# RMSNorm and QKV projection on one core: another load order, another opening schedule, and the last two tiles stored by column chunk

## The chip, the cores and the metric

The kernel runs on one core of a Trainium2 chip. The core has a matrix engine (TensorE, in the profile PE for matmuls and PEld for weight loads), a vector engine (VectorE, DVE), a scalar engine (ScalarE, ACT), GpSimd (POOL) and a queue engine (SyncE, SP) that issues nearly all of this kernel's transfers. Every engine works through its own list of instructions in order; semaphores make one wait for another. Transfers from SP's queue are carried out by 16 DMA engines.

The metric is the device time of one execution in microseconds (us). A number of executions give a median.

## The reference, cut to what matters

```python
batch, n_heads, seq, head_dim = 8, 12, 1024, 64
dim = n_heads * head_dim                     # 768
x      (8, 1024, 768) f32;  gamma (768,);  w_qkv (768, 2304);  eps 1e-5

rms = np.sqrt(np.mean(x ** 2, axis=-1, keepdims=True) + eps)
x_norm = x / rms * gamma
return np.matmul(x_norm, w_qkv).astype(np.float32)
```

Each of the 8192 rows of x is divided by its root mean square, multiplied by gamma by column, and multiplied by a 768 by 2304 matrix.

## The kernel before, in words

**Tiling.** The 8192 rows are 64 x tiles of 128 rows. The inner dimension of 768 is six K blocks of 128. The 2304 output columns are four chunks of 512 and one of 256, at columns 0, 512, 1024, 1536 and 2048. One output chunk of one x tile is six matmuls that add up in one PSUM buffer; one x tile is 30 matmuls, the whole kernel 1920. Matmuls take bf16; x and the weights come as f32.

**Where the norm is done.** gamma is multiplied into the weights while they are converted to bf16 (`conv`, lines 160 to 168, on VectorE, ScalarE or GpSimd). The division by the root mean square is done when a chunk leaves PSUM (`evac`, lines 235 to 245, on VectorE or ScalarE): each row is multiplied by its reciprocal. `stat` (lines 180 to 186, ScalarE) sums the squares and takes the root, and `recip` (line 190, VectorE) inverts it.

**Transposing x.** A matmul needs x with its columns on the partitions. There are three ways in the kernel:

- `tr_half` and `cp_half` (lines 206 to 215), as `trA`, `trB`, `cpA`, `cpB` in the plan: TensorE transposes the f32 tile in two parts (K blocks 0 to 3, and 4 and 5), and VectorE or ScalarE copies them to bf16.
- `cast`, `tr` and `cp` (lines 176 to 200): VectorE casts the tile to bf16, TensorE transposes all six blocks, VectorE or ScalarE copies them out of PSUM.
- `cast` and `xbar` (line 219): VectorE casts, and SP issues a transfer that transposes.

Before, tiles 0 to 2 go the first way, tile 3 the second, and all others the third.

**Pieces of the weights.** The weights are loaded in 12 pieces. `PIECES` (line 12) gives each piece's first and last K block, first column and width. For columns 0 to 511 there is a piece of two K blocks and four of one; for 512 to 2047 pieces of three K blocks (768 KB); the last 256 columns are one piece. A piece lies in a staging buffer until all its K blocks are converted; pieces of one shape share up to four buffers (lines 115 and 157).

**The head.** The first six x tiles (`HEAD = 6`) are worked on together while the weights arrive. Their order is written out by hand: `HEAD_PLAN` (line 28) holds lines of a planned time, an operation, its arguments and an engine. `("mm", 0, 512, "345")` is: x tile 0, the chunk at column 512, K blocks 3, 4, 5. `LOADS` (line 17) holds the loads: `"w"` with a piece's number, `"x"` with a tile's, and `"t"`, the transposing transfer of a tile. All operations are sorted by planned time and then emitted (lines 316 and 317); the times set nothing but this order in each engine's list. `idle(n)` emits n matmuls on zeros (lines 275 to 278).

**After the head.** The other 58 tiles follow in a loop (lines 301 to 314): load, cast, transposing transfer, statistics, then 30 matmuls and five evictions, on VectorE and ScalarE in turn.

**Queues and buffers.** SP's queue holds every load of x and of weights, every transposing transfer and every store, in the order of the plan. Eight semaphores serve them in turn, so a transfer is issued only when the one eight places ahead of it has landed. All PSUM tiles, those of the transposes and the idle matmuls too, come from one pool of eight buffers in turn (line 128).

**Stores.** `evac_at` (lines 265 to 273) plans an eviction and its store. A tile's output is stored in three parts, `PARTS` (line 118): columns 0 to 1023, 1024 to 2047, and 2048 to 2303, each when all of its chunks are evicted. The last tile is stored chunk by chunk. In the head a store is planned at least 1.0 after its eviction and not before 21.85, just after the last entry of `LOADS`.

Of the kernel before, what the change touches and what calls it, by code (L numbers as in the profile page):

```python
# [8 lines left out]


HEAD = 6
PIECES = [(0, 2, 0, 512), (2, 3, 0, 512), (3, 4, 0, 512), (4, 5, 0, 512), (5, 6, 0, 512), (0, 3,
          512, 512), (3, 6, 512, 512), (0, 3, 1024, 512), (3, 6, 1024, 512), (0, 3, 1536, 512),
          (3, 6, 1536, 512), (0, 6, 2048, 256)]


LOADS = [
    (-9.00, "w", 0), (-8.99, "x", 0), (-8.98, "x", 1), (-8.97, "x", 2), (-8.96, "w", 1),
    (-8.95, "w", 2), (-8.94, "x", 3), (-8.93, "w", 3), (-8.92, "w", 4), (-8.91, "w", 5),
    (-8.90, "w", 6), (-8.89, "x", 4), (-8.88, "w", 7), (-8.87, "w", 8), (-8.86, "x", 5),  # L20
    (16.69, "t", 4), (16.70, "w", 9), (21.71, "t", 5), (21.72, "w", 10), (21.73, "w", 11),
    (21.74, "x", 6), (21.75, "x", 7),
]

EARLY = 3


HEAD_PLAN = [
    (4.99, "conv", 0, 0, "ACT"), (4.99, "conv", 0, 1, "DVE"), (5.95, "trA", 0), (5.99, "stat", 0),
    (6.82, "trB", 0), (7.04, "trB", 1), (7.25, "trA", 1), (7.26, "idle", 3), (7.38, "recip", 0),  # L30
    (7.39, "cpB", 1, "ACT"), (7.54, "cpA", 0, "DVE"), (7.83, "cpA", 1, "ACT"), (7.94, "trB", 2),
    (8.16, "trA", 2), (8.30, "cpB", 2, "DVE"), (8.45, "cpB", 0, "ACT"), (8.59, "mm", 0, 0, "01"),
    (8.70, "conv", 1, 2, "DVE"), (8.81, "stat", 2), (9.02, "mm", 1, 0, "01"),
    (9.18, "cpA", 2, "DVE"), (9.32, "conv", 2, 3, "POOL"), (9.45, "mm", 0, 0, "2"),
    (9.67, "mm", 1, 0, "2"), (9.92, "mm", 2, 0, "012"), (10.31, "cast", 3, "DVE"),
    (10.31, "stat", 3), (10.56, "mm", 0, 0, "3"), (10.78, "mm", 1, 0, "3"), (10.86, "recip", 2),
    (10.99, "mm", 2, 0, "3"), (11.02, "conv", 3, 4, "DVE"), (11.21, "tr", 3),
    (11.56, "mm", 0, 0, "4"), (11.65, "conv", 4, 5, "DVE"), (11.69, "cp", 3, "ACT"),
    (11.78, "mm", 1, 0, "4"), (12.00, "mm", 2, 0, "4"), (12.13, "recip", 3),
    (12.21, "mm", 0, 0, "5"), (12.43, "mm", 1, 0, "5"), (12.54, "stat", 1),  # L40
    (12.59, "evac", 0, 0, "DVE"), (12.64, "mm", 3, 0, "01234"), (13.67, "conv", 5, 0, "DVE"),
    (13.67, "conv", 5, 1, "POOL"), (13.72, "mm", 2, 0, "5"), (13.94, "mm", 3, 0, "5"),
    (14.10, "evac", 2, 0, "ACT"), (14.15, "recip", 1), (14.21, "mm", 0, 512, "0"),
    (14.31, "evac", 3, 0, "DVE"), (14.42, "mm", 1, 512, "0"), (14.62, "conv", 5, 2, "POOL"),
    (14.64, "mm", 2, 512, "0"), (14.79, "evac", 1, 0, "ACT"), (14.85, "mm", 0, 512, "1"),
    (15.07, "mm", 1, 512, "1"), (15.28, "mm", 2, 512, "1"), (15.50, "mm", 3, 512, "0"),
    (15.68, "conv", 6, 3, "DVE"), (15.68, "conv", 6, 4, "POOL"), (15.68, "conv", 6, 5, "ACT"),
    (15.72, "mm", 0, 512, "2"), (15.93, "mm", 1, 512, "2"), (16.15, "mm", 2, 512, "2"),
    (16.36, "mm", 3, 512, "12"), (16.67, "cast", 4, "DVE"), (16.67, "stat", 4),
    (16.80, "mm", 0, 512, "345"), (17.44, "mm", 1, 512, "345"), (18.06, "recip", 4),  # L50
    (18.09, "mm", 2, 512, "345"), (18.25, "evac", 1, 512, "ACT"), (18.68, "conv", 7, 0, "DVE"),
    (18.74, "mm", 3, 512, "345"), (18.94, "conv", 7, 1, "ACT"), (19.16, "conv", 7, 2, "DVE"),
    (19.39, "mm", 0, 1024, "0"), (19.60, "mm", 1, 1024, "0"), (19.64, "evac", 2, 512, "DVE"),
    (19.65, "evac", 3, 512, "ACT"), (19.82, "mm", 0, 1024, "12"), (20.25, "mm", 1, 1024, "12"),
    (20.39, "evac", 0, 512, "DVE"), (20.68, "mm", 2, 1024, "012"), (20.70, "conv", 8, 3, "ACT"),
    (20.70, "conv", 8, 4, "POOL"), (21.33, "mm", 3, 1024, "012"), (21.69, "cast", 5, "DVE"),
    (21.69, "stat", 5), (21.97, "mm", 0, 1024, "34"), (22.41, "mm", 1, 1024, "34"),
    (22.84, "mm", 4, 0, "012345"), (23.02, "conv", 8, 5, "ACT"), (23.08, "recip", 5),
    (24.13, "mm", 4, 512, "012345"), (24.29, "evac", 4, 0, "DVE"), (24.65, "conv", 9, 0, "POOL"),
    (24.65, "conv", 9, 1, "ACT"), (25.36, "conv", 9, 2, "ACT"), (25.43, "mm", 4, 1024, "012"),  # L60
    (25.59, "evac", 4, 512, "DVE"), (26.07, "mm", 0, 1024, "5"), (26.29, "mm", 1, 1024, "5"),
    (26.45, "evac", 0, 1024, "DVE"), (26.51, "mm", 2, 1024, "345"),
    (26.67, "evac", 1, 1024, "ACT"), (27.15, "mm", 3, 1024, "345"),
    (27.31, "evac", 2, 1024, "DVE"), (27.80, "mm", 4, 1024, "345"),
    (27.96, "evac", 3, 1024, "ACT"), (28.45, "mm", 5, 0, "012345"),
    (28.65, "evac", 4, 1024, "ACT"), (29.25, "conv", 10, 3, "POOL"),
    (29.25, "conv", 10, 5, "DVE"), (29.74, "mm", 5, 512, "012345"), (29.90, "evac", 5, 0, "DVE"),
    (30.20, "conv", 10, 4, "POOL"), (31.04, "mm", 5, 1024, "012345"),
    (31.20, "evac", 5, 512, "DVE"), (31.64, "conv", 11, 0, "ACT"), (31.64, "conv", 11, 4, "POOL"),
    (31.95, "conv", 11, 2, "DVE"), (32.12, "conv", 11, 5, "ACT"), (32.25, "conv", 11, 3, "DVE"),  # L70
    (32.33, "mm", 0, 1536, "012"), (32.55, "evac", 5, 1024, "DVE"), (32.98, "mm", 1, 1536, "012"),
    (33.30, "conv", 11, 1, "DVE"), (33.63, "mm", 2, 1536, "012"), (34.28, "mm", 3, 1536, "012"),
    (34.92, "mm", 4, 1536, "012"), (35.57, "mm", 5, 1536, "012"), (36.22, "mm", 0, 1536, "345"),
    (36.86, "mm", 1, 1536, "345"), (37.02, "evac", 0, 1536, "DVE"), (37.51, "mm", 2, 1536, "345"),
    (37.67, "evac", 1, 1536, "ACT"), (38.16, "mm", 3, 1536, "345"),
    (38.32, "evac", 2, 1536, "DVE"), (38.81, "mm", 4, 1536, "345"),
    (38.97, "evac", 3, 1536, "ACT"), (39.45, "mm", 5, 1536, "345"),
    (39.61, "evac", 4, 1536, "DVE"), (40.10, "mm", 0, 2048, "012345"),
    (40.26, "evac", 5, 1536, "ACT"), (40.76, "mm", 1, 2048, "012345"),
    (40.92, "evac", 0, 2048, "DVE"), (41.41, "mm", 2, 2048, "012345"),  # L80
    (41.57, "evac", 1, 2048, "DVE"), (42.07, "mm", 3, 2048, "012345"),
    (42.23, "evac", 2, 2048, "DVE"), (42.72, "mm", 4, 2048, "012345"),
    (42.88, "evac", 3, 2048, "DVE"), (43.38, "mm", 5, 2048, "012345"),
    (43.54, "evac", 4, 2048, "DVE"), (44.19, "evac", 5, 2048, "DVE"),
]
HEAD_END = 44.03


@with_exitstack
def kernel(  # L90
# [21 lines left out]
    MT = M // P  # L112
    NT = 512
    inv_k = 1.0 / float(K)
    PIECE_BUFS = {(k1 - k0, n): min(4, sum((q[1] - q[0], q[3]) == (k1 - k0, n) for q in PIECES))
                  for k0, k1, _, n in PIECES}

# [37 lines left out]
    def load_w(c):  # L155
        k0, k1, n0, n = PIECES[c]
        WF[c] = wst.tile([P, k1 - k0, n], f32, name=f"w_f{k1 - k0}_{n}", bufs=PIECE_BUFS[k1 - k0, n])
        nc.sync.dma_start(out=WF[c], in_=wv[:, k0:k1, n0:n0 + n])  # L158

    def conv(c, ko, eng):  # L160
        k0, k1, n0, n = PIECES[c]
        o, i, g = w_b[:, ko, n0:n0 + n], WF[c][:, ko - k0, :], g_sb[:, ko:ko + 1]
        if eng == "DVE":
            nc.vector.tensor_scalar(out=o, in0=i, scalar1=g, scalar2=None, op0=mult)  # L164
        elif eng == "ACT":
            nc.scalar.activation(out=o, in_=i, func=AF.Copy, scale=g, bias=0.0)  # L166
        else:
            nc.gpsimd.tensor_scalar(out=o, in0=i, scalar1=g, scalar2=1.0, op0=mult, op1=mult)  # L168
# [86 lines left out]
    def at(time, fn, *args):  # L255
        plan.append((time, len(plan), fn, args))
# [8 lines left out]
    def evac_at(time, t, n0, eng, gap):  # L265
        at(time, evac, t, n0, eng)
        h = part(n0)
        nl = min(NT, N - n0)
        left[t, h] = left.get((t, h), PARTS[h][1]) - nl
        if t == MT - 1:  # L270
            at(time + gap - 0.5, store, t, h, n0, nl)
        elif left[t, h] == 0:
            at(time + gap, store, t, h, *PARTS[h])
# [8 lines left out]
        at(time, {"x": load_x, "w": load_w, "t": xbar}[kind], n)  # L282
    at(0.0, idle, 18)
    at(2.8, gamma_in)
    at(2.81, idle, 28)
    ops = {"conv": conv, "cast": cast, "stat": stat, "recip": recip, "tr": tr, "cp": cp, "mm": mm, "idle": idle}
    for time, op, *args in HEAD_PLAN:
        if op == "evac":
# [10 lines left out]
    US = 6 * 0.2158 / 512  # L299
    now, flip = HEAD_END, 0  # L300
    for t in range(HEAD, MT):
# [51 lines left out]
```

## Time and profile before

| what | value |
|---|---|
| median of 7 executions | 389.51 us (389.13 to 389.89) |
| the profiled execution's own time | 389.73 us |
| its span, first to last instruction | 387.9 us |
| TensorE busy with matmuls | 379.8 us (98%) |
| VectorE, ScalarE, GpSimd busy | 153.9, 181.1, 7.5 us |
| moved by DMA | 119.91 MB, mean 309 GB/s |
| granted TensorE clock over the span | 1.000 |

The profile is of one execution. In a timeline, a line gives the start and the time that a group took, the engine and line of the kernel, the operation, what it writes and reads, how many there are, and in brackets how long the engine was idle before it and what ended that. Matmuls are pipelined: the time of a group holds a tail after its last start. "SPq" and the like are an engine's sequencer, which issues transfers. The chain that ended last is followed back from the last instruction, at each step to what released it. Some matmul records are missing from a trace.

### The profile page before, as it was taken

What the parts mean: (1) busy time and instruction counts of PE and PEld (TensorE: products, weight loads), DVE (VectorE), ACT (ScalarE), POOL (GpSimd) and SP (SyncE); (2) the same over time, 40 slices, a digit from 0 to 9 for tenths busy, and PEclk for the clock granted to TensorE, in tenths of its full rate; (3) what the DMA queues carried; (4) which work ended last, traced back from release to release, by engine and by line L of the source; (5) the groups of instructions that cost most, each with busy time, mean ns of one, the idle gap of its engine ahead of it and who ended that gap; (6) DMA issues with size and microseconds to landing.
All of it is one profiled execution on the core that took longest, in us unless ns stands there. A gap on an engine that the chain in (4) does not pass through costs nothing.

```text
span 387.9 us, 5512 instructions
## 1 busy us (share of the span) xinstructions
PE 379.8 (98%) x1956; PEld 195.1 (50%) x1994; DVE 153.9 (40%) x309; ACT 181.1 (47%) x362; POOL 7.5 (2%) x15
## 2 busy tenths in 40 slices
PE   8999999999999999999999999999999999999995
PEld 7444654554554554554554554554554554554552
DVE  2655524444333344333343433343433343433331
ACT  4762444444544444444444444544444544444531
POOL 0312000000000000000000000000000000000000
PEclk9999999999999999999999999999999999999999
DMA  8999999999999999999999999999999999999964
GB/s 269 390 277 383 325 373 336 384 344 329 329 284 316 288 313 306 290 325 306 291 311 293 309 318 304 289 314 306 304 276 338 302 308 299 270 341 294 297 241 190
DMA packets 89223, 119.91 MB, mean 309 GB/s; under 512 B 52326, under 2 KB 61292, under 8 KB 89196
## 3 DMA queue, kind: packets, MB, share of 16 engines
q1 hardware_dynamic: 89184, 119.56, 100.8%
q8 instruction: 15, 0.25, 0.3%
q14 instruction: 12, 0.10, 0.1%
q10 hardware_dynamic: 12, 0.00, 0.0%
HBM read 32.25 MB, written 75.50 MB: 278 GB/s over the span
## 4 chain that ended last, share of the span: by engine, by line
PE 93%; DMA 4%; issue 1%; SPq 0%; DVE 0%; ACT 0%
PE pm L229 93%; DMA w_f<-in_w_qkv_dram 4%; SPq L153 0%; DVE w_b L164 0%; ACT ot L245 0%; SPq L158 0%
## 5 line engine op out<-in xcount | busy, mean ns | idle before, releaser
L229 PE MATMUL pm<-w_b,xT 128*128 128x512 bf16 (+1 forms) x1882 | 371.9, 357 | 2.2 <-DVE w_b L164 0.2
L229 PEld LDWEIGHTS <-xT 128*128 128x128 bf16 x1920 | 187.7, 98 | 185.8 <-issue 0.5
L243 DVE TENSOR_SCALAR ot<-pm,rstd 128x512 f32<-128x512 f32 (+1 forms) x165 | 113.6, 694 | 200.4 <-PE pm L229 200.0
L245 ACT ACTIVATE ot<-pm,rstd 128x512 f32<-128x512 f32 (+1 forms) x155 | 100.2, 647 | 190.8 <-PE pm L229 154.5
L183 ACT ACTIVATE sq<-x_t 128x768 bf16<-128x768 f32 x64 | 53.4, 835 | 1.6 <-DMA x_t<-in_x_dram 1.6
L172 DVE CAST xb<-x_t 128x768 bf16<-128x768 f32 x61 | 33.2, 545 | 18.9 <-DMA x_t<-in_x_dram 18.9
L185 ACT ACTIVATE rms<-ssq,eps_sb 128x1 f32<-128x1 f32 x64 | 18.8, 294 | 2.1
L183 ACT ACTIVATION_READ_ACCUMULATOR sq<-x_t 128x1 f32 x64 | 12.3, 192 | 0.0
L190 DVE RECIPROCAL rstd<-rms 128x1 f32<-128x1 f32 x64 | 9.8, 154 | 3.2 <-ACT rms L185 3.2
L166 ACT ACTIVATE w_b<-w_f,g_sb 128x512 bf16<-128x512 f32 (+1 forms) x9 | 5.8, 669 | 5.3 <-DMA w_f<-in_w_qkv_dram 5.3
L168 POOL TENSOR_SCALAR w_b<-w_f,g_sb 128x512 bf16<-128x512 f32 (+1 forms) x9 | 6.8, 765 | 24.8 <-DMA w_f<-in_w_qkv_dram 15.8
L278 PE MATMUL pm<-warm 128*128 128x128 bf16 x49 | 5.5, 305 | 1.0 <-DVE eps_sb L137 1.0
L164 DVE TENSOR_SCALAR w_b<-w_f,g_sb 128x512 bf16<-128x512 f32 (+1 forms) x12 | 5.2, 450 | 2.9 <-DMA w_f<-in_w_qkv_dram 2.8
L278 PEld LDWEIGHTS <-warm 128*128 128x128 bf16 x49 | 5.0, 144 | 1.0 <-DVE eps_sb L137 1.0
L210 PE MATMUL pm<-ident_f,x_t 128*128 128x128 f32 x18 | 2.5, 277 | 0.9 <-DMA x_t<-in_x_dram 0.9
L210 PEld LDWEIGHTS pm<-ident_f,x_t 128*128 128x128 f32 x18 | 1.9, 141 | 1.3 <-DMA x_t<-in_x_dram 1.2
L172 DVE CAST xT<-pm 128x512 bf16<-128x512 f32 (+1 forms) x3 | 1.8, 600 | 1.9 <-PE pm L210 1.9
L174 ACT CAST xT<-pm 128x256 bf16<-128x256 f32 (+1 forms) x3 | 1.2, 445 | 1.8 <-PE pm L210 1.7
L140 ACT ACT_TABLE_LOAD x1 | 1.3, 1283 | 1.4 <-PEq L334 1.4
L174 ACT COPY xT<-pm 128x768 bf16<-128x768 bf16 x1 | 0.8, 798 | 0.3 <-PE pm L196 0.3
L261 DVE COPY g_sb<-pm 128x6 f32<-128x6 f32 x1 | 0.2, 164 | 1.8 <-PE pm L260 1.8
L196 PEld LDWEIGHTS <-xb 128*128 128x128 bf16 x6 | 0.4, 98 | 0.2
(13 smaller groups left out, 2.4 us busy)
## 6 DMA issues: line engine op xcount, KB each, us to landing
out_dram<-ot SPq DMA_DIRECT2D x126, 512.0 KB, 3.8
x_t<-in_x_dram SPq DMA_DIRECT2D x64, 384.0 KB, 4.1
out_dram<-ot SPq DMA_DIRECT2D x64, 128.0 KB, 3.2
w_f<-in_w_qkv_dram SPq DMA_DIRECT2D x7, 768.0 KB, 8.7
w_f<-in_w_qkv_dram SPq DMA_DIRECT2D x4, 256.0 KB, 7.0
out_dram<-ot SPq DMA_DIRECT2D x4, 256.0 KB, 2.0
xT<-xb SPq DMA_TRANSPOSE x60, 4.3
w_f<-in_w_qkv_dram SPq DMA_DIRECT2D x1, 512.0 KB, 3.7
```

The lines of the kernel that those rows point to most:

```text
L164: nc.vector.tensor_scalar(out=o, in0=i, scalar1=g, scalar2=None, op0=mult)
L166: nc.scalar.activation(out=o, in_=i, func=AF.Copy, scale=g, bias=0.0)
L168: nc.gpsimd.tensor_scalar(out=o, in0=i, scalar1=g, scalar2=1.0, op0=mult, op1=mult)
L172: nc.vector.tensor_copy(out=out, in_=in_)
L183: nc.scalar.activation(out=sq, in_=X[t], func=AF.Square, accum_out=ssq)
L185: nc.scalar.activation(out=rms, in_=ssq, func=AF.Sqrt, scale=inv_k, bias=eps_sb)
L190: nc.vector.reciprocal(out=r, in_=RS[t])
L210: nc.tensor.transpose(out=PT[t, h][:, ko - k0, :], in_=X[t][:, ko * P:(ko + 1) * P], identity=ident_f)
L229: nc.tensor.matmul(out=PM[t, n0][:, :nl], lhsT=XT[t][:, ko, :], rhs=w_b[:, ko, n0:n0 + nl], start=(b == 1), stop=(b == KO))
L243: nc.vector.tensor_scalar(out=o, in0=pm[:, :nl], scalar1=RS[t], scalar2=None, op0=mult)
L245: nc.scalar.activation(out=o, in_=pm[:, :nl], func=AF.Copy, scale=RS[t], bias=0.0)
L278: nc.tensor.matmul(out=wps, lhsT=warm, rhs=warm, start=True, stop=True)
```

## The change

The change replaces the tables of the head, lets x tiles 4 and 5 be transposed by TensorE, and stores one more tile by chunk. No function of the arithmetic is changed.

- **Load order.** x tiles 0 and 1 are loaded before the first piece of weights; x tile 3 moves ahead of piece 2. All head loads, x 6 and 7 too, stand at the front of SP's list; the two `"t"` entries are gone.
- **Pieces.** Columns 512 to 1023 come as three pieces of two K blocks (512 KB) instead of two of three. There are 13 pieces; no shape has more pieces than staging buffers, except that three-block pieces now number four, for four buffers.
- **Head order.** A new `HEAD_PLAN`: statistics of tiles 0 and 1 at once, first conversions on ScalarE and GpSimd, x tile 2's transposes between the first matmuls, tile 3's copy on VectorE, and `tr` and `cp` for tiles 4 and 5 (on VectorE and ScalarE).
- **Idle matmuls.** 28 after gamma's become 9, and 3 before the first matmuls become 13.
- **Stores.** The last two tiles, not the last one alone, are stored chunk by chunk. With the last entry of `LOADS` at -8.80, head stores are planned 1.0 after their eviction.

```diff
-PIECES = [(0, 2, 0, 512), (2, 3, 0, 512), (3, 4, 0, 512), (4, 5, 0, 512), (5, 6, 0, 512), (0, 3,
-          512, 512), (3, 6, 512, 512), (0, 3, 1024, 512), (3, 6, 1024, 512), (0, 3, 1536, 512),
-          (3, 6, 1536, 512), (0, 6, 2048, 256)]
+PIECES = [(0, 2, 0, 512), (2, 3, 0, 512), (3, 4, 0, 512), (4, 5, 0, 512), (5, 6, 0, 512), (0, 2,
+          512, 512), (2, 4, 512, 512), (4, 6, 512, 512), (0, 3, 1024, 512), (3, 6, 1024, 512), (0,
+          3, 1536, 512), (3, 6, 1536, 512), (0, 6, 2048, 256)]

 LOADS = [
-    (-9.00, "w", 0), (-8.99, "x", 0), (-8.98, "x", 1), (-8.97, "x", 2), (-8.96, "w", 1),
-    (-8.95, "w", 2), (-8.94, "x", 3), (-8.93, "w", 3), (-8.92, "w", 4), (-8.91, "w", 5),
-    (-8.90, "w", 6), (-8.89, "x", 4), (-8.88, "w", 7), (-8.87, "w", 8), (-8.86, "x", 5),
-    (16.69, "t", 4), (16.70, "w", 9), (21.71, "t", 5), (21.72, "w", 10), (21.73, "w", 11),
-    (21.74, "x", 6), (21.75, "x", 7),
+    (-9.00, "x", 0), (-8.99, "x", 1), (-8.98, "w", 0), (-8.97, "x", 2), (-8.96, "w", 1),
+    (-8.95, "x", 3), (-8.94, "w", 2), (-8.93, "w", 3), (-8.92, "w", 4), (-8.91, "w", 5),
+    (-8.90, "w", 6), (-8.89, "x", 4), (-8.88, "w", 7), (-8.87, "w", 8), (-8.86, "w", 9),
+    (-8.85, "x", 5), (-8.84, "w", 10), (-8.83, "w", 11), (-8.82, "w", 12), (-8.81, "x", 6),
+    (-8.80, "x", 7),
 ]
 HEAD_PLAN = [
+    (4.00, "stat", 0), (4.00, "trA", 0), (4.87, "trB", 0), (5.01, "cpA", 0, "DVE"),
+    (5.31, "trB", 1), (5.33, "stat", 1), (5.69, "cpB", 0, "DVE"), (5.74, "trA", 1),
+    (5.75, "idle", 13), (6.09, "cpB", 1, "DVE"), (6.49, "recip", 0), (6.72, "recip", 1),
+    (6.83, "conv", 0, 0, "ACT"), (6.83, "conv", 0, 1, "POOL"), (6.88, "cpA", 1, "DVE"),
+    (7.60, "mm", 0, 0, "0"), (7.82, "trA", 2), (7.83, "stat", 2), (8.25, "mm", 0, 0, "1"),
+    (8.39, "cpA", 2, "DVE"), (8.47, "mm", 1, 0, "01"), (8.50, "conv", 1, 2, "POOL"),
+    (8.90, "trB", 2), (9.13, "mm", 2, 0, "01"), (9.22, "recip", 2), (9.26, "cpB", 2, "ACT"),
+    (9.49, "cast", 3, "DVE"), (9.57, "mm", 0, 0, "2"), (9.62, "stat", 3), (9.78, "mm", 1, 0, "2"),
+    (10.00, "mm", 2, 0, "2"), (10.16, "conv", 2, 3, "DVE"), (10.21, "tr", 3),
+    (10.70, "mm", 0, 0, "3"), (10.83, "conv", 3, 4, "DVE"), (10.92, "mm", 1, 0, "3"),
+    (11.14, "mm", 2, 0, "3"), (11.31, "cp", 3, "DVE"), (11.37, "mm", 0, 0, "4"),
+    (11.59, "mm", 1, 0, "4"), (11.81, "mm", 2, 0, "4"), (11.87, "recip", 3),
+    (12.02, "mm", 3, 0, "01234"), (12.03, "conv", 4, 5, "DVE"), (12.85, "conv", 5, 0, "DVE"),
+    (13.10, "mm", 0, 0, "5"), (13.32, "mm", 1, 0, "5"), (13.33, "conv", 5, 1, "DVE"),
...
+    (14.40, "mm", 1, 512, "01"), (14.56, "conv", 6, 2, "DVE"), (14.83, "mm", 2, 512, "01"),
+    (14.86, "evac", 3, 0, "ACT"), (15.04, "conv", 6, 3, "DVE"), (15.26, "mm", 3, 512, "01"),
+    (15.52, "cast", 4, "DVE"), (15.55, "stat", 4), (15.69, "mm", 0, 512, "23"),
+    (16.12, "mm", 1, 512, "2"), (16.34, "tr", 4), (16.67, "mm", 1, 512, "3"),
+    (16.81, "cp", 4, "DVE"), (16.89, "mm", 2, 512, "23"), (17.32, "mm", 3, 512, "23"),
+    (17.37, "recip", 4), (17.42, "conv", 7, 5, "ACT"), (17.53, "conv", 7, 4, "DVE"),
+    (17.75, "mm", 4, 0, "012345"), (19.05, "mm", 4, 512, "0123"), (19.21, "evac", 4, 0, "DVE"),
+    (19.91, "mm", 0, 512, "45"), (19.96, "conv", 8, 2, "DVE"), (20.34, "mm", 1, 512, "45"),
...
+    (22.40, "conv", 9, 3, "POOL"), (22.57, "stat", 5), (22.72, "mm", 1, 1024, "012"),
+    (22.98, "cast", 5, "DVE"), (23.36, "mm", 2, 1024, "01"), (23.79, "tr", 5),
+    (23.90, "conv", 9, 4, "ACT"), (23.96, "recip", 5), (24.13, "mm", 2, 1024, "2"),
+    (24.35, "mm", 3, 1024, "012"), (24.45, "conv", 10, 2, "DVE"), (24.61, "cp", 5, "ACT"),
...
-HEAD_END = 44.03
+HEAD_END = 44.46
...
-        if t == MT - 1:
+        if t >= MT - 2:
             at(time + gap - 0.5, store, t, h, n0, nl)
...
-    at(2.81, idle, 28)
+    at(2.81, idle, 9)
```

## The prediction

> **What bounds the kernel now.** I read the chain that ended last first, then the matmul engine's timeline, then the queue's and the other engines' timelines over the head.
>
> The page's chain, and pieces of the chain in order of time (start, us, what):
>
> ```profile
> PE 93%; DMA 4%; issue 1%; SPq 0%; DVE 0%; ACT 0%
> ...
> 9.49 10.63 DMA w_f<-in_w_qkv_dram
> 20.12 0.03 issue
> 20.15 0.50 DVE w_b L164
> 20.64 0.04 issue
> 20.69 10.30 PE pm L229 x47
> ...
> 55.92 9.46 PE pm L229 x49
> 65.38 0.05 issue
> 65.43 9.46 PE pm L229 x49
> 74.89 0.05 issue
> 74.94 10.10 PE pm L229 x49
> ...
> 383.96 0.47 ACT ot L245
> ```
>
> Until 20.15 us weight loads end the chain, from 20.69 on only matmuls do. The three blocks from 55.92 to 85.09 are 29.17 us; with one record lost per block (1,882 records against 1,920 weight loads) they are 150 matmuls, five x tiles of 30, so a tile is 5.834 us and 64 tiles are 373.4 us. The same blocks repeat to the end, so there is no steady stall to win. TensorE's timeline over the head:
>
> ```profile
> 3.22 3.08 PE L278 MATMUL pm<-warm 128*128 128x128 bf16 x28
> 6.14 0.82 PE L210 MATMUL pm<-ident_f,x_t 128*128 128x128 f32 x6
> 7.90 0.87 PE L210 MATMUL pm<-ident_f,x_t 128*128 128x128 f32 x6 [0.93 <-DMA x_t<-in_x_dram]
> 8.61 0.33 PE L278 MATMUL pm<-warm 128*128 128x128 bf16 x3
> 8.93 0.85 PE L210 MATMUL pm<-ident_f,x_t 128*128 128x128 f32 x6
> 9.62 2.75 PE L229 MATMUL pm<-w_b,xT 128*128 128x512 bf16 x11
> 12.21 0.50 PE L196 MATMUL pm<-ident,xb 128*128 128x128 bf16 x6
> 12.54 7.93 PE L229 MATMUL pm<-w_b,xT 128*128 128x512 bf16 x35
> 20.69 29.56 PE L229 MATMUL pm<-w_b,xT 128*128 128x512 bf16 x152 [0.21 <-DVE w_b L164]
> ```
>
> Real matmuls begin at 9.62. After that only two things stand between them: tile 3's six transposes (12.21 to 12.54, 0.335) and one wait for piece 7. The last matmul before it starts near 20.10 and needs 0.216 (29.17/5, less six 256-wide ones at half the time, over 24: 5.834/27), so 20.31 to 20.69 is 0.38 lost. The account closes: 9.62 + 373.4 + 0.34 + 0.38 = 383.7, and the last eviction starts at 383.96. The span is 387.9 and its run 389.73, 0.22 above the median of 389.51; I count differences on the profiled execution and add them to the median.
>
> **When loads land.** With eight loads out, a load issues when the one eight places ahead has landed, so issue starts and waits give landings: w0 4.48 (ACT's first conversion), x0 5.37, x1 7.87, x2 8.81, w1 9.49, w2 10.17, x3 11.14, w3 at most 11.83, w4 12.52, w5 14.55, w6 16.55, x4 18.11, w7 20.14, w8 22.15, x5 23.11. I lay these against KB asked for so far (x 384, pieces 512, 256 or 768). The new order has the same totals at many places: x1 768 KB, by interpolation 5.1; w0 1280, 7.87; x2 1664, 8.81; w1 1920, 9.49; x3 2304, 10.5; w2 2560, 11.14; w3 2816, 11.8; w4 12.5; w5 3584, 13.9; w6 4096, 15.2; x4 16.2; w7 4992, 18.1; w8 20.1; w9 22.15; x5 23.1.
>
> **The change part by part.**
>
> *Order of loads and the first matmuls.* x0 and x1 are squared and transposed before w0 lands. Then ACT's conversion (0.72) gives block 0 at 8.59, and with 0.05 to TensorE (20.64 to 20.69 in the chain) the first matmul is at 8.65, not 9.62. GpSimd converts block 1 (0.69, longest row 0.99: at worst 8.9) and block 2 (9.55 to 10.24, at worst 10.54). TensorE does one matmul, 0.44 of x2's transposes, three matmuls, 0.22 of transposes to 10.24; VectorE's copy of x2's first half ends at 10.23, so the next five matmuls run 10.28 to 11.36, tile 3's transposes to 11.69 and, after w2's conversion (11.2 to 11.68), three more to 12.38. The conversion of w3 (11.87 to 12.35) opens block 4 at 12.40. At that point both kernels have done the same: x0 to x2 on blocks 0 to 3, and tile 3 transposed. Before reaches it at 12.54. So most of the 0.97 us at the first matmul is lost again to x2's transposes in the stream (0.66) and to the wait for w3: gain 0.14.
>
> *Tile 3's copy moves from ACT (0.80) to VectorE,* behind w3's conversion. No row has this copy on VectorE. Bounds: 0.56, the cast of as many elements from SBUF; and 0.955, from 0.69 for 512 and 0.425 for 256 f32 elements out of PSUM. I take 0.80, the same tile's row, between them: 12.35 to 13.15, when TensorE is free at 13.05, so 0.15 lost (0.56 loses nothing, 0.955 loses 0.30). VectorE's conversions of blocks 4 and 5 queue behind it, to 13.79: TensorE wants them at 14.28.
>
> [...]
>
> *Tiles 4 and 5 by TensorE.* Two more sets of six transposes in the stream: 2 x 0.335 = 0.67 lost. Their casts are ready: x4 lands at 16.2, cast by 17.3, transposes wanted at 17.5; x5 at 23.1, cast after two evictions by 24.8, wanted near 25.0. This is the thinnest cover; if VectorE is one 0.75 eviction later, up to 0.6 is added.
>
> *Two queue transposes removed.* In before, SP waits from 12.24 to 18.70 for tile 4's cast, and piece 9 stands behind it. This view by stage (PE, PEld, DVE, ACT, POOL, then clock, DMA share, GB/s) shows the price:
>
> ```profile
> 5.00:10.00 5.00, 4.06 (x36) 3.48 (x35) 1.43 (x4) 3.00 (x8) 0.00 (x0) 1.00 0.99 345
> 10.00:15.00 5.00, 4.95 (x28) 2.37 (x28) 3.68 (x10) 3.95 (x10) 1.08 (x2) 1.00 1.05 394
> 20.00:25.00 5.00, 4.79 (x22) 2.03 (x21) 2.92 (x6) 3.86 (x7) 0.69 (x1) 1.00 1.17 269
> 25.00:30.00 5.00, 5.00 (x25) 2.28 (x24) 3.22 (x5) 2.72 (x5) 0.85 (x2) 1.00 0.95 287
> ```
>
> From 20 to 30 the rate falls from 394 to 269 and 287. Yet TensorE is full there, so faster loads win nothing; worth 0. All 21 new loads issue with no buffer wait, and head stores, no longer held to 21.85, queue behind them.
>
> *Pieces of two blocks.* w7 lands at 18.1 and is wanted near 21, since tile 4's matmuls come first: the 0.38 stall goes. Next in line are w6's conversions, ready at 16.6 against 16.9; covered by 0.3.
>
> *Stores by chunk for the last two tiles.* Two more issues of 0.33 in SP's queue while it idles (next store at 380.14); the last tile's stores were in chunks already. From 370 to 380 the DMA share is 0.66, so nothing queues: 0, with ends of -0.2 (a larger store out of the way) and +0.2.
>
> Sum: -0.14 + 0.15 + 0.67 - 0.38 = **+0.30 us**: profiled 390.03, on the median 389.8, or +0.08%. A measurement here tells about 0.2% (0.78 us) from no change, so I forecast no change.
>
> **The rivals.**
>
> *Cold clock (slower).* Warm-up matmuls go from 28 + 3 to 9 + 13, with transposes between. In before the 28 take 3.08 us (0.11 each) and the later 3 only 0.33 with a pipeline tail of 0.22, so full speed came near 6.1, 5.1 us after TensorE's start. If full speed is not reached by 8.65 and needs about that long from there, 4 to 5 us run at half speed: 2.0 to 2.5 lost, less 0.17 of waiting; with +0.30, 391.6 to 392.1. It decides once the cold stretch after 8.65 passes 1.3 us. Against it: from 6.14 to 9.62 before ran almost only transposes and stayed at speed.
>
> [...]
>
> *Loads without the early lag (faster).* x1 took from 5.37 to 7.87 where x0 took 0.89. At the later 394 GB/s the stage from 5 to 10 would need 4.38 us: 0.62 earlier, hence +0.30 - 0.62, 389.2. With no lag at all x1's total lands at 6.26, 1.6 earlier; TensorE's own work then limits, block 4 opens near 11.0, and it is 388.4. For it: the rows show the lag only before 9 us, so it belongs to the start, which is what is reordered. Against: the same bytes are asked for at the same times.
>
> *VectorE late (slightly slower).* It now takes copies 3 and 4 and more conversions. Copy at 0.955 adds 0.15, tile 5's cast 0.6, and one eviction in front of w6's conversion 0.4: 390.0 to 390.9.
>
> **How the numbers follow.** Forecast 0.52, cold clock 0.13, loads earlier 0.2, VectorE late 0.15. Beyond 0.2% lie most of the earlier loads' far half (faster 0.15), the cold clock, half of VectorE late and 0.07 of unplanned waits in the forecast's tail (slower 0.28); 0.57 is left within. The range 388.8 to 391.0 leaves out the far ends of the first two rivals. The forecast's own range is 389.4 to 390.3.
>
> **What would show it.** First real matmul near 8.65, block 4 of x0 near 12.4, three groups of L196 transposes, no wait for weights after 13, tile 6 starting about 0.3 later, L174 or L172 rows for the copies. Wrong if warm-up spacing (0.11) goes on past 8.65, if weights land a microsecond off, or if TensorE has gaps between 13 and 45.

## The result and the profile after

| | before | after |
|---|---|---|
| median time, us | 389.3 (389.02 to 389.89, 38 executions) | 390.22 (389.57 to 392.37, 16 executions) |
| ratio | | 1.0025 (1.0018 to 1.0032) |
| the profiled execution: time / span | 389.73 / 387.94 | 390.0 / 387.85 |
| median span | 387.7 (102 executions of the later series) | 388.05 (28 executions of both) |
| time outside the span, mean | 1.79 | 2.11 |

The changed kernel is slower by 0.25%, about 0.9 us. A second series of the same two kernels gave 1.0016 (1.0007 to 1.0024). Both medians lie in the range, 0.2 to 0.4 above the forecast of 389.8; a loss beyond the 0.2% that the forecast kept to was measured in the first series, and one within it in the second. The two profiled spans differ by 0.1 only, the other way, and that is the puzzle that the runs below had to solve. The median spans differ by 0.35. By series it is less even: in the second the median spans differ by 0.1 (387.7 and 387.8); in the first, whose spans of before were not kept, times less the 1.79 and 2.11 outside the span differ by some 0.6.

The page's chain of the changed kernel, as shares of the span:

```profile
PE 96%; DMA 2%; issue 1%; ACT 0%; SPq 0%; ACTq 0%
```

The weight loads' share fell from 4 to 2: after 13 us no load ends the chain any more. TensorE's timeline over the head of the changed kernel (start, us, what, and in brackets the idle time ahead):

```profile
4.21 2.77 PE L210 MATMUL pm<-ident_f,x_t 128*128 128x128 f32 x12
6.78 1.15 PE L278 MATMUL pm<-warm 128*128 128x128 bf16 x13
8.41 0.38 PE L229 MATMUL pm<-w_b,xT 128*128 128x512 bf16 x1 [0.48 <-ACT w_b L166]
...
11.11 0.50 PE L196 MATMUL pm<-ident,xb 128*128 128x128 bf16 x6
11.55 5.77 PE L229 MATMUL pm<-w_b,xT 128*128 128x512 bf16 x26
17.16 0.50 PE L196 MATMUL pm<-ident,xb 128*128 128x128 bf16 x6
17.49 7.29 PE L229 MATMUL pm<-w_b,xT 128*128 128x512 bf16 x32
24.61 0.50 PE L196 MATMUL pm<-ident,xb 128*128 128x128 bf16 x6
24.95 25.25 PE L229 MATMUL pm<-w_b,xT 128*128 128x512 bf16 x131
```

The first real matmul is at 8.41, tiles 0 and 1 are transposed before it, there are three groups of six bf16 transposes, and the wait for piece 7 at 20.5 is gone. By stage (PE, PEld, DVE, ACT, POOL, then clock, DMA share, GB/s) the changed kernel shows

```profile
5.00:10.00 5.00, 4.47 (x32) 3.71 (x31) 2.91 (x8) 3.30 (x8) 1.34 (x2) 1.00 0.98 326
10.00:15.00 5.00, 5.00 (x28) 2.44 (x28) 3.81 (x10) 2.16 (x6) 0.04 (x1) 1.00 1.05 396
20.00:25.00 5.00, 5.00 (x30) 2.40 (x28) 4.12 (x8) 3.24 (x7) 1.36 (x2) 1.00 1.04 389
```

From 20 to 25 the loads run at 389 GB/s where before had 269. TensorE is full in both (5.00 against 4.79, and the 0.21 is the wait for piece 7), so the 120 GB/s buy nothing else.

**Where the time went.** From the first real matmul to the last one's start there are 373.33 us of matmuls, plus the transposes that stand between them, plus waits, which are what is left over; where a gap shows in TensorE's records, it agrees with them. Then come the tail (last matmul's start to the end of the span) and the time outside the span. In us:

| trace | first matmul | transposes in the stream | waits | sum of the three | tail | outside, mean of its executions |
|---|---|---|---|---|---|---|
| before | 9.62 | 0.34 | 0.38 | 10.3 | 4.29 | 1.79 |
| before, again | 9.45 | 0.34 | 0.65 | 10.4 | 4.28 | 1.80 |
| before, two tiles by chunk (part 3) | 8.97 | 0.34 | 1.32 | 10.6 | 3.91 | 1.80 |
| before, two by chunk and softer lead (part 6) | 8.69 | 0.34 | 0.97 | 10.0 | 3.94 | 1.78 |
| after | 8.41 | 1.66 | 0.20 | 10.3 | 4.25 | 2.11 |
| after, again | 7.85 | 1.66 | 0.72 | 10.2 | 4.26 | 2.13 |
| after, gamma later (part 2) | 8.98 | 1.66 | 0.19 | 10.8 | 4.27 | 2.11 |
| after, one tile by chunk (part 3) | 9.39 | 1.66 | 0.18 | 11.2 | 4.26 | 2.14 |
| after, three tiles by chunk (part 3) | 8.55 | 1.66 | 0.38 | 10.6 | 3.78 | 2.14 |

Two things are to be seen. In the kernel before, more than half of an earlier first matmul is lost again, because pieces 6 and 7 land when they land: as the first matmul goes from 9.62 over 9.45 and 8.97 to 8.69, the waits for them grow from 0.38 over 0.54 and 0.80 to 0.97. The rest of the waits, 0.1 in the repeat and 0.5 with two tiles by chunk, is at tile 11 near 74 us. TensorE's timeline in the kernel of part 6 has two waits for piece 6:

```profile
11.61 5.34 PE L229 MATMUL pm<-w_b,xT 128*128 128x512 bf16 x24
17.32 0.38 PE L229 MATMUL pm<-w_b,xT 128*128 128x512 bf16 x1 [0.36 <-DVE w_b L164]
17.87 2.32 PE L229 MATMUL pm<-w_b,xT 128*128 128x512 bf16 x9 [0.18 <-POOL w_b L168]
```

In the changed kernel no wait for weights is left after 13 us, so from 8.41 to 9.39 the first matmul moves the end one for one, and the sums go from 10.3 to 11.2; the earliest, at 7.85, loses its lead again to waits for x tile 2 and for tile 5's cast. That fits the spread of the executions: 1.4 us in the changed kernel (one at 392.37 left out), and in the kernel before 0.9 in the first two series, 1.0 (one at 391.73 left out) and 1.2 in the others. And the last column has a step of 0.32 that belongs to no stage of the head at all.

### The profile page after: what moved, and what is told of

It reads as the page before. It is cut to its first block, busy times and chain, and to the rows that moved or that the text cites. A ratio compares the mean times of both kernels' runs of the same rounds, so it can differ in the third digit from the quotient of the medians.

```text
span 387.9 us, 5519 instructions
## 1 busy us (share of the span) xinstructions
PE 380.3 (98%) x1958; PEld 195.9 (50%) x1997; DVE 157.0 (40%) x315; ACT 178.0 (46%) x357; POOL 7.3 (2%) x16
## 4 chain that ended last, share of the span: by engine, by line
PE 96%; DMA 2%; issue 1%; ACT 0%; SPq 0%; ACTq 0%
PE pm L229 96%; DMA w_f<-in_w_qkv_dram 2%; PE pm L196 0%; PE pm L210 0%; SPq L153 0%; ACT w_b L166 0%; ACT ot L245 0%; ACTq L166 0%
## 5 line engine op out<-in xcount | busy, mean ns | idle before, releaser
L164 DVE TENSOR_SCALAR w_b<-w_f,g_sb 128x512 bf16<-128x512 f32 (+1 forms) x15 | 6.6, 472 | 2.1 <-DMA w_f<-in_w_qkv_dram 2.0
L278 PE MATMUL pm<-warm 128*128 128x128 bf16 x40 | 4.4, 293 | 1.0 <-DVE eps_sb L137 1.0
L278 PEld LDWEIGHTS <-warm 128*128 128x128 bf16 x40 | 3.8, 138 | 1.1 <-DVE eps_sb L137 1.0
L172 DVE CAST xT<-pm 128x512 bf16<-128x512 f32 (+1 forms) x5 | 2.7, 581 | 3.5 <-PE pm L210 3.5
L210 PE MATMUL pm<-ident_f,x_t 128*128 128x128 f32 x18 | 3.8, 372 | 0.1
L210 PEld LDWEIGHTS pm<-ident_f,x_t 128*128 128x128 f32 x18 | 3.2, 200 | 1.0 <-DMA x_t<-in_x_dram 0.8
L166 ACT ACTIVATE w_b<-w_f,g_sb 128x512 bf16<-128x512 f32 (+1 forms) x5 | 3.1, 630 | 1.3 <-DMA w_f<-in_w_qkv_dram 1.3
L196 PEld LDWEIGHTS <-xb 128*128 128x128 bf16 x18 | 1.2, 98 | 0.7 <-DVE xb L172 0.3
L172 DVE COPY xT<-pm 128x768 bf16<-128x768 bf16 x2 | 1.1, 554 | 1.1 <-PE pm L196 1.1
L196 PE MATMUL pm<-ident,xb 128*128 128x128 bf16 x18 | 1.5, 219 | 0.0
```

The lines of the kernel that those rows point to most:

```text
L172: nc.vector.tensor_copy(out=out, in_=in_)
L210: nc.tensor.transpose(out=PT[t, h][:, ko - k0, :], in_=X[t][:, ko * P:(ko + 1) * P], identity=ident_f)
L278: nc.tensor.matmul(out=wps, lhsT=warm, rhs=warm, start=True, stop=True)
```

## The experiments

Ratios are to the kernel before, on the same chip, with a 95% interval. Its median was 389.49 in the first two groups (35 executions each) and 389.52 in the third (32).

**1. Both kernels again, unchanged.** No edit.

> The kernel before, unchanged, to have its span in every execution beside its time. Outside theory: its time exceeds its span by 1.8 us, as in the one profiled execution, where the changed kernel's exceeds it by 2.0 to 2.2; then 0.3 of the 0.9 us lies outside the span. If the difference is the same for both kernels, nothing lies there. Stream and clock theories say nothing on this. Times 389.0 to 389.9.

> The changed kernel, unchanged, for a second profile and more spans. Stream theory (a fixed loss: two more sets of transposes, 0.67 us, less a smaller wait for weights): median 390.2, spread like before's 0.9 us, TensorE dense after 13 us. Clock theory (full clock comes at a time that differs from execution to execution): spread over 2 us, and in slow executions matmuls 0.43 us apart after 8.4 us.

The kernel before: 389.6, ratio 1.0003 (0.9994 to 1.0011). The changed kernel: 389.97, ratio 1.0016 (1.0007 to 1.0024). Time outside the span was 1.80 (1.76 to 1.82 over 11 executions) and 2.13 (2.07 to 2.19 over 11): the two do not overlap, so some 0.3 us of the loss is in every execution of the changed kernel and in no engine's stream. The changed kernel's trace lost 0.16 at tile 5's cast, the cover that the prediction called the thinnest.

**2. Is it the clock?** One kernel gives the warm-up a stretch without a hole, by emitting gamma's small transpose later:

```diff
-    at(2.8, gamma_in)
+    at(5.5, gamma_in)
```

> The changed kernel with gamma's transpose moved from between the idle matmuls to between the transposes of x tiles 0 and 1, so that TensorE has no 0.45 us hole at 2.8 us and is busy without one from 1.0 to 7.8. Clock theory: full clock comes sooner or more surely, the spread shrinks to about 1 us and the median falls by 0.2 to 0.6. Stream theory: median within 0.2 of the changed kernel's.

Another takes away the idle matmuls ahead of the first real one:

```diff
-    (5.75, "idle", 13), (6.09, "cpB", 1, "DVE"),
+    (5.75, "idle", 1), (6.09, "cpB", 1, "DVE"),
```

> The changed kernel with 1 idle matmul in place of 13 before the first matmul, so that TensorE stands still from about 6.9 to 8.4 us. Clock theory: more executions start the matmuls at half speed; median up by 0.5 to 2 us, some executions at 392 or above. Stream theory: no change within 0.2 us, since the idle matmuls end before the weights come.

Gamma later: 390.49 (389.58 to 392.85), ratio 1.0026 (1.0011 to 1.004). The trace has the full clock from 4.29 instead of 7.32, and nothing is won: in these traces the clock is full before the first real matmul, so a cold clock is not what the changed kernel loses by in most executions. The earlier clock need not come from the edit, for a kernel of part 3 with the unedited opening has it from 4.37; and one execution, at 392.85, still had a mean clock of 0.993. One idle matmul: 391.16 (389.39 to 393.28), ratio 1.0045 (1.0027 to 1.0064), with 7 of 12 executions at 391.1 or more. Its TensorE timeline and its stages (columns as above) show the rival at work:

```profile
5.81 0.22 PE L278 MATMUL pm<-warm 128*128 128x128 bf16 x1
8.88 0.58 PE L229 MATMUL pm<-w_b,xT 128*128 128x512 bf16 x1 [2.85 <-ACT w_b L166]
```

```profile
5.00:10.00 5.00, 2.14 (x13) 1.73 (x13) 2.08 (x6) 3.02 (x7) 0.94 (x2) 0.78 1.00 345
10.00:15.00 5.00, 4.78 (x19) 2.52 (x19) 2.29 (x6) 1.80 (x5) 0.44 (x1) 0.54 1.05 395
```

In this trace TensorE idles 2.85 us, the granted clock falls to half from 7.79 to 14.62, and TensorE starts 19 matmuls and transposes from 10 to 15 where the changed kernel starts 28. The 7 executions at 391.1 or more have mean clocks of 0.990 to 0.996, the other five (389.39 to 390.24) 0.998 to 1.000. So the cold-clock rival is real in this kernel and costs 1 to 3.5 us when it strikes; with the 13 idle matmuls it stays away in 27 of 28 executions of the changed kernel (the one at 392.37 had a mean clock of 0.996).

**3. The stores by chunk, alone and taken away.** The edit on the kernel before, and its reverse on the changed one:

```diff
-        if t == MT - 1:
+        if t >= MT - 2:
```

> The kernel before with one edit of the change alone: the last two tiles stored by chunk. In the runs so far the time exceeds the span by 1.79 us in the kernel before and by 2.11 in the changed one and in its two variants. Tail theory: the two more stores put this 0.32 us there; time minus span 2.11, median 389.8. Head theory: it comes from the other edits; time minus span 1.79, median 389.5. My prediction had 0 for this edit.

> The changed kernel with the last tile alone stored by chunk, as before. Tail theory: time minus span falls from 2.11 to 1.79, median about 389.8. Head theory: stays 2.11, median 390.0 to 390.2.

On the kernel before: 389.13 (388.75 to 389.68), ratio 0.9987 (0.9977 to 0.9997), a gain of 0.36. Taken away from the changed kernel: 390.13, ratio 1.0019 (1.0005 to 1.0034), no difference from the changed kernel. The gain sits in the tail: 3.91 instead of 4.28. It is not the transfer, since the last eviction ends 0.78 after the last matmul's start and the last store lands 2.80 to 2.88 after it in each of these. It is what SP does afterwards. SP pauses for 0.34 to 0.36 us before its 592nd recorded instruction, whatever that instruction is: in 11 of the 14 traces this stands alone, in the other three SP waits there anyway, for 0.97 to 1.23. The pause comes back every 128 instructions: 0.43 to 0.46 us before the 80th and 0.34 to 0.35 before the 208th, 336th and 464th in all 14 traces. The kernel before has 597 on SP, and the pause comes after the last landing; with two tiles by chunk it has 601, the 592nd instruction stands four places further from the end of the list, and the pause can pass while SP waits for the stores. SP's waits, in the kernel before and in this one (us, times, longest):

```profile
SPq L348 <- DMA out_dram<-ot: 1.6, 1, 1.6
```

```profile
SPq L348 <- DMA out_dram<-ot: 1.6, 2, 1.2
```

In the first the closing wait stands whole ahead of the 592nd instruction. In the second the last two stores are waited for by the 592nd and 593rd, and the pause passes within the first of these waits, 1.2 long. The changed kernel has 600, one too few: its pause runs from 2.86 to 3.20, just after the landing at 2.82. If that reading is right, one more tile by chunk should hide it there too:

```diff
-        if t >= MT - 2:
+        if t >= MT - 3:
```

> The changed kernel with the last three tiles stored by chunk instead of two, which gives SP about four more instructions. In every trace so far SP pauses 0.34 to 0.41 us before its 592nd recorded instruction. Where that instruction comes after the last store's landing (before, the changed kernel, the changed kernel with one tile by chunk) the span ends about 4.26 after the last matmul's start; where it comes while SP waits for that landing anyway (before with two tiles by chunk) 3.9. Pause theory: here it falls into the wait, tail 3.9, median 0.35 below the changed kernel (389.7). Rival: the stores by chunk themselves set the tail; then the changed kernel with one, two or three tiles by chunk is the same, 390.1.

389.54 (388.93 to 390.0), ratio 1.0001 (0.9992 to 1.0011): level with the kernel before. SP has 604 instructions, the tail is 3.78 instead of 4.26, and its span's median 387.4 instead of 388.05. The tail explains 0.48; the rest is of the size that the head's own spread can make of a median.

**4. Tiles 4 and 5 by TensorE.** The changed kernel with tile 5 transposed by the queue again:

```diff
-    (-8.85, "x", 5), (-8.84, "w", 10), (-8.83, "w", 11), (-8.82, "w", 12), (-8.81, "x", 6),
-    (-8.80, "x", 7),
+    (-8.85, "x", 5), (-8.84, "w", 10), (23.60, "t", 5), (23.61, "w", 11), (23.62, "w", 12),
+    (23.63, "x", 6), (23.64, "x", 7),
...
-    (22.98, "cast", 5, "DVE"), (23.36, "mm", 2, 1024, "01"), (23.79, "tr", 5),
+    (22.98, "cast", 5, "DVE"), (23.36, "mm", 2, 1024, "01"),
...
-    (24.35, "mm", 3, 1024, "012"), (24.45, "conv", 10, 2, "DVE"), (24.61, "cp", 5, "ACT"),
+    (24.35, "mm", 3, 1024, "012"), (24.45, "conv", 10, 2, "DVE"),
```

> The changed kernel with tile 5 transposed in SP's queue again, its transfer set between pieces 10 and 11, so that one of the two new sets of transposes leaves TensorE. Stream theory: 0.335 us less in the stream, median 0.3 below the changed kernel's (389.7 to 389.9). Rival: the queue's transpose costs DMA time that weights or tile 5 then miss: tile 5's first matmuls wait, no gain or a loss of up to 1 us.

390.21 (389.82 to 391.02), ratio 1.0016 (1.0004 to 1.0027): no gain. The transposes in the stream fall from 1.66 to 1.33, as priced. But the queue pays for it, by stage and then in a wait near 74 us (us, times, longest):

```profile
20.00:25.00 5.00, 5.00 (x24) 2.25 (x23) 4.20 (x9) 3.40 (x7) 1.58 (x2) 1.00 0.64 241
```

```profile
PEld L229 <- DMA xT<-xb: 1.5, 1, 1.5
```

The rate from 20 to 25 falls from 389 to 241 GB/s, and at tile 11, where the loop's lead drops, TensorE waits for the transposing transfer (1.42 us lost in the stream). The changed kernel and its repeat have no such wait. This trace is of the second slowest of the 12 executions, 390.99; what the others lose there was not traced. (This trace's tail is 3.88 with 600 instructions on SP: its last store is waited for one instruction later than in the changed kernel, so the pause passes while that store is still out.)

**5. The kernel before with piece 7 one place earlier.** The cheapest way to take away the wait for piece 7, with tile 4's load and its cast, statistics and transfer moved behind:

```diff
-    (-8.90, "w", 6), (-8.89, "x", 4), (-8.88, "w", 7), (-8.87, "w", 8), (-8.86, "x", 5),
-    (16.69, "t", 4), (16.70, "w", 9), (21.71, "t", 5), (21.72, "w", 10), (21.73, "w", 11),
+    (-8.90, "w", 6), (-8.89, "w", 7), (-8.88, "x", 4), (-8.87, "w", 8), (-8.86, "x", 5),
+    (19.64, "t", 4), (19.65, "w", 9), (21.71, "t", 5), (21.72, "w", 10), (21.73, "w", 11),
...
-    (16.36, "mm", 3, 512, "12"), (16.67, "cast", 4, "DVE"), (16.67, "stat", 4),
+    (16.36, "mm", 3, 512, "12"),
...
-    (19.39, "mm", 0, 1024, "0"), (19.60, "mm", 1, 1024, "0"), (19.64, "evac", 2, 512, "DVE"),
+    (19.39, "mm", 0, 1024, "0"), (19.60, "mm", 1, 1024, "0"), (19.63, "cast", 4, "DVE"), (19.64, "evac", 2, 512, "DVE"),
...
```

> The kernel before with piece 7 loaded ahead of x tile 4, and tile 4's cast, statistics and queue transpose moved after the first conversions of piece 7. This takes away before's one wait for weights (0.38 and 0.54 us in its two profiles), which is the only saving that the change's stream has against its own added transposes. Stream theory: 0.3 to 0.5 us below before, 389.0. Rival: tile 4's transpose, now issued about 2 us later, lands later than 23.8 and its matmuls wait instead: no gain, or slower.

390.28 (389.48 to 391.82), ratio 1.0023 (1.0009 to 1.0038): slower. The wait for piece 7 is gone, as in the changed kernel; TensorE's timeline and the stage from 20 to 25 show what came instead:

```profile
17.64 0.38 PE L229 MATMUL pm<-w_b,xT 128*128 128x512 bf16 x1 [0.77 <-DVE w_b L164]
18.20 8.04 PE L229 MATMUL pm<-w_b,xT 128*128 128x512 bf16 x35 [0.18 <-POOL w_b L168]
```

```profile
20.00:25.00 5.00, 4.95 (x24) 2.17 (x24) 2.77 (x7) 4.92 (x11) 0.69 (x1) 1.00 0.70 159
```

The early first matmul (8.61) ran into waits for piece 6 instead, 1.27 us in all; the kernels of parts 3 and 6, with their early starts, lose 0.80 and 0.87 there. With `("t", 4)` planned at 19.64 the loads from 20 to 25 fell to 159 GB/s, which cost the stream 0.1 in that stage, and 0.5 is lost at tile 11. The sum of the three is 10.9, some 0.5 above the other traces of before. One trace does not say how much of this the edit did; it does show that a stall taken out of a stream that is bound by arrival need not shorten it.

**6. The best of the kernel before.** Two tiles by chunk, and the loop's lead let down over three tiles rather than at once, against the wait at tile 11:

```diff
-        if t == MT - 1:
+        if t >= MT - 2:
...
-        ahead = 6.0 if t < HEAD + 5 else 0.0
+        ahead = 6.0 if t < HEAD + 5 else max(0.0, 4.5 - 1.5 * (t - HEAD - 5))
```

> The kernel before with the last two tiles stored by chunk and with the lead of the cast and queue transpose falling by 1.5 us a tile from tile 11 on, instead of from 6.0 to 0 at once. In traces of the kernel before and two variants tile 11's matmuls wait 0.3 to 0.7 us near 74 us for that transpose; in four traces of the changed kernel and its variants they do not. Backlog theory: this wait belongs to the step in the lead; it goes, and the median falls 0.2 to 0.5 below before with two tiles by chunk (389.1), to 388.6 to 388.9. Rival: the transposes issued earlier push stores and x loads back and another tile waits: no gain.

389.14 (388.65 to 389.71), ratio 0.9989 (0.998 to 0.9998): the wait at tile 11 is gone from the trace, and the median is that of the chunk stores alone (389.13). The wait is not in most executions, or is given back; nothing more was won.

**7. What is the 0.32 outside the span?** Between the two kernels the number of recorded instructions on an engine differs: GpSimd 31 before and 32 after, VectorE 435 and 439, ScalarE 490 and 485. SP's number is not it: with 601 on the kernel before the time outside was 1.80, with 596 on the changed one 2.14 (part 3). So the kernel before with one more fill on GpSimd, and with four more on VectorE, on a buffer that nothing reads:

```diff
+    spare = singles.tile([P, 1], f32)
+    nc.gpsimd.memset(spare, 0.0)
```

> The kernel before with one more small fill on GpSimd at the start, so that GpSimd has 32 recorded instructions like the changed kernel, not 31. It tells where the 0.32 us outside the span come from. If from GpSimd's count: time minus span 2.11, median 389.8. If not: 1.79, median 389.5.

```diff
+    spare = singles.tile([P, 4], f32)
+    for i in range(4):
+        nc.vector.memset(spare[:, i:i + 1], 0.0)
```

> The kernel before with four small fills more on VectorE at the start, so that VectorE has 439 recorded instructions like the changed kernel, not 435. If the 0.32 us outside the span come from VectorE's count: time minus span 2.11. If not: 1.79, and with the run on GpSimd also at 1.79 the cause stays open between ScalarE's count and the head's order.

One more on GpSimd: 388.73 (388.54 to 389.22), ratio 0.9981 (0.9971 to 0.999), outside the span 1.81. Four more on VectorE: 389.12 (388.76 to 389.86), ratio 0.9997 (0.9988 to 1.0007), outside the span 2.14 (2.11 to 2.16). It is VectorE's list: at 435 and 437 instructions (before and its variants) the time outside is 1.78 to 1.81, at 439 and 440 (after and its variants, and this kernel) 2.11 to 2.15. What happens at that count, no record shows. The changed kernel with four fewer on VectorE was not tried.

Both kernels were faster *in* the span, by 0.7 (median 386.9 and 387.0 against 387.7), which nobody had asked of a fill. By stage, the kernel of part 6, without the extra buffer, and the one with a fill on GpSimd:

```profile
10.00:15.00 5.00, 5.00 (x29) 2.41 (x29) 3.58 (x9) 3.97 (x9) 1.41 (x3) 1.00 1.06 390
15.00:20.00 5.00, 4.41 (x20) 1.85 (x19) 1.55 (x5) 3.25 (x7) 1.32 (x2) 1.00 1.03 384
```

```profile
10.00:15.00 5.00, 5.00 (x29) 2.40 (x28) 3.64 (x9) 4.05 (x9) 1.61 (x2) 1.00 1.06 410
15.00:20.00 5.00, 4.66 (x22) 2.07 (x22) 2.07 (x7) 3.58 (x8) 0.99 (x1) 1.00 1.04 403
```

From 10 to 20 us the loads run at 403 to 411 GB/s in both kernels with the buffer, and at 383 to 397 in those without it. Their waits in the stream are 0.45 and 0.14, with first matmuls at 8.54 and 8.55, so the sums of the three are 9.3 and 9.0. From 10 to 20 us packets of 2048 bytes take 84 ns on average instead of 87 to 88, and the median of those of 3072 bytes is 121 instead of 126. In the kernel before, the medians are 86 and 126 ns from 10 to 20 us, 84 and 121 from 3 to 8, and that of 3072 bytes is 121 from 60 to 370, so its packets are longer from 10 to 20 us and not in those stretches. The two kernels share an extra buffer and its fills; which of these shortens the packets, and how, no run shows. The kernel with one fill is the best of all that ran, 0.8 us under the kernel before; with the chunk stores on top it was not run.

## Why the prediction was right, and where it was wrong

**The sum of the stream: right, as far as this can be measured.** By the table's sums, the four traces of before and of its variants in tail and loop average 10.3, the five of after and its variants 10.6. That is +0.3, with sums that differ by up to 1.0 among traces of one stream, and the median spans give +0.35, from 0.1 in one series and some 0.6 in the other; the forecast was +0.30. That the two agree to a few hundredths is luck. The profiled pair alone gives nothing: its execution of before had a span 0.24 above its median, that of after one 0.2 below.

**Its terms, one by one.** First matmul: 8.65 forecast, 8.41 in the profile, 7.85 to 9.39 over five traces, 8.64 on average. Block 4 opening at 12.40 instead of 12.54: it opened near 12.2, with x2's transposes and the conversions falling in the order written. Transposes of tiles 4 and 5 at 0.335 each: measured. Wait for piece 7, 0.38: gone. The queue transposes worth nothing, with the rate rising from 269 to 389 GB/s and TensorE full in both: measured, and part 4 shows what putting one back costs. VectorE's timeline in the changed kernel has the three steps that were in doubt:

```profile
12.00 0.55 DVE L172 COPY xT<-pm 128x768 bf16<-128x768 bf16 x1
...
17.69 0.56 DVE L172 COPY xT<-pm 128x768 bf16<-128x768 bf16 x1 [1.13 <-PE pm L196]
...
23.76 0.74 DVE L172 CAST xb<-x_t 128x768 bf16<-128x768 f32 x1
```

**Tile 3's copy: mis-sized.** It was taken at 0.80 with 0.15 lost; it takes 0.55, and tile 4's 0.56, and loses nothing. That is the lower of the two bounds, the cast of as many elements from SBUF at 0.56. The nearest row on another engine was the wrong neighbour. Against that, tile 5's cast, 0.74 long in this trace, took 0.83 in two of six traces and made TensorE wait 0.16 and 0.19. Where it does so, the two errors, both near 0.15, cancel.

**Cold clock: rightly a rival, rightly small.** It did not strike in the profile, and in about one of 28 executions; part 2 gives its price, 1 to 3.5, somewhat more than the 1.8 to 2.3 forecast. In the changed kernel's profile the clock came to full at 7.32, after idle matmuls up to 4.21 and mostly f32 transposes from there; the idle matmuls around it start 0.107 us apart before and 0.056 after.

**Loads without the early lag: a spread, not a gain.** The start varies by execution more than by order: the first matmul lies between 7.85 and 9.39 in five traces of the changed order, 8.64 on average, and between 8.69 and 9.62 in four of the old one, 9.18 on average. What was missed is that the waits for pieces 6 and 7, which the change removes, had been absorbing part of that.

**VectorE late, the copy at 0.955:** refuted by the row above; of the 0.6 that it allowed for tile 5's cast, at most 0.19 was seen.

**The step that failed: what lies around the span.** The working took 389.73 less 387.9, that is 1.8, as the same for both kernels and summed only steps of the stream. It rose by 0.32. With +0.35 in the spans that is +0.67, and the two series measured +0.5 and +0.9 in their medians. No row of the profile before could have given it, but it is more than any single term of the sum apart from the added transposes and the wait for piece 7, and it turns "no change" into a loss that can just be measured. The stores by chunk were put at 0 with ends of ±0.2; on the kernel before they are worth -0.36, on the changed kernel 0, and the reason is not a transfer that is out of the way but where SP's pause falls. So the 0 came true in the changed kernel by the accident of its 600 instructions.

## What to carry to other kernels

A wait that ends on an arrival hid part of every delay ahead of it: in the kernel before, the waits for pieces 6 and 7 grew from 0.38 to 0.97 as the first matmul came 0.93 earlier. In the changed kernel, with those waits gone, the start of the stream set the end one for one, the sums going from 10.3 to 11.2 as the first matmul went from 8.41 to 9.39, so ask what varies there before you count such a wait as won. Trust an average over many executions for the sum and a trace for its terms: here the two profiled spans stood 0.2 off their medians, in opposite directions, and hid the change in the span. Where a change is worth tenths of a microsecond, look outside the span too, at the tail of the queue engine and at what an unused buffer does, for these moved the time (by 0.36 and 0.8 on the kernel before) as much as a hand-made schedule of the head.

## What the runs showed of the hardware that was not expected

- **A fixed pause in SP's list, every 128 recorded instructions.** 0.43 to 0.46 us before the 80th, 0.34 to 0.36 before the 208th, 336th, 464th and 592nd, hidden where SP waits just then. A tile more by chunk moves the end of the list against it. Some 0.6 us after the 592nd starts, the trace has a packet of 8192 bytes of the kind that the profile calls "instruction" (387.08 and 387.70 in the kernel before, 386.81 and 387.46 in the changed one), which the author read as the loading of the list; no run shows that, and what SP waits for is not settled.
- **VectorE's number of instructions counts outside the span.** 439 or 440 instead of 435 or 437 cost 0.33 us, with four fills of a few bytes as with the change's own; the cause is not settled.
- **A fill more, on a buffer that nothing reads, went with faster loads.** From 10 to 20 us, 403 to 411 GB/s in the two kernels with one, 383 to 397 in the others, whose packets were 4 to 5% longer there (87 to 88 ns on average against 84 for 2048 bytes, medians of 126 against 121 for 3072). In the kernel before, the medians from 3 to 8 us are 84 and 121. The cause is not settled.
- **The clock's changes came in steps of 3.41 us.** The records of granted clock last 3.41 us (full, from 4.38 to 7.79 in the kernel with one idle matmul), 6.83 (half, to 14.62) and, full to the end of the work, 378.88 in the changed kernel and 382.29 in the kernel before, which are 111 and 112 times 3.413. The phase differs from execution to execution: full clock first comes between 4.29 and 7.34 in the 14 traces. That would explain that the same hole in TensorE's work costs time in 7 of 12 executions of the kernel with one idle matmul and not in the others; that was not tried by itself.
